# Gates of 64 more tokens through two small tables, and the gate loads issued by ScalarE

## The chip, the cores and the metric

The kernel runs on 1 core of one Trainium2 chip. The metric is the device time of one execution in microseconds (us), the median of several runs. The profile is one execution, recorded by the hardware profiler.

A core has five engines with a queue each, which run in parallel and wait for each other through semaphores: TensorE (PE in the profile; PEld are its weight loads), VectorE (DVE), ScalarE (ACT), GpSimd (POOL) and SyncE (SP), which here only issues DMAs. SyncE, ScalarE and GpSimd can issue DMAs; an issue takes its turn in the queue of its engine.

## The reference

A trunk of two layers over 256 tokens of 1024 channels, in float32. Layer 0 mixes tokens by a gated short convolution, layer 1 by windowed attention; after each mixer stands a PEER block, which is where nearly all of the time goes. A PEER block finds, for each token, 8 heads x 16 experts out of 16384, by the best sums of two sub-key scores, and computes

```python
idx = ...                                   # 128 experts per token, number i1 * 128 + i2
g = softmax(top_v, axis=-1)                 # 16 gates per head
h = einsum("cd,ced->ce", x, u_tab[idx])
a = g * gelu(h)
out = einsum("ce,ced->cd", a, v_tab[idx])
```

## The kernel before

**The PEER block is computed densely.** For all 16384 experts and all 256 tokens, `h = u x` is formed on TensorE (the tiles `ph`), GELU follows, the result is multiplied by a gate that is zero where the token did not choose the expert, and the product with `v` sums over the experts (the tiles `pv`). An expert has the number 128 i1 + i2; i1 is the partition and i2 = j the tile: tile j holds the experts of one i2 for all 256 tokens. `halves` are two buffers of 64 tiles each, `hm` for j below 64 ("half 0") and the routing scratch `sc` for j from 64 on ("half 1"), which by then is no longer needed for routing. In the profile they are called `hm` and `route`.

**Weights.** Each tile of 128 x 1024 float32 comes in through SyncE (`raw`, 4 buffers), ScalarE rounds it to `hi` (line 179, 3 buffers), VectorE forms the rest `lo` (line 180, 2 buffers). `take` and `prefetch` keep one tile ahead. Products of the parts give float32 precision: `wide_product`, `cols_product` for u, and `rows_product` for v, with 12 products of 512 columns per tile of v.

**Two ways for the gates.** For the first 128 tokens ("first tile") the gates are added into a table in device memory, `table`, 128 x 16384 with the cell (i1, i2, token): `sent` computes the places, and `scatter` (line 474) issues 16 indirect DMAs per head on GpSimd, 128 per layer, each with one cell per token. The DMAs of a head wait for those of the head before. The table is first blanked by `blank_table` (line 461), 8 transfers of 1 MB per layer on GpSimd, each waiting for the one before; in layer 0 that begins in the convolution, in layer 1 at the end of the first PEER block. The sub-keys `subk` (line 663) are loaded by GpSimd too, once the buffer `HB` is free. During the product with v, `load_gates` (line 922) loads the gates of two tiles from the table through GpSimd into one of 2 buffers, and `gated` (line 934) multiplies them in on VectorE.

For the other 128 tokens ("second tile") there is no table: `one_hots` (lines 855 to 859) forms one-hot rows of i1 and of i2 with the gate in three bfloat16 parts, for 8 tokens at a time, and `spread` multiplies them on TensorE (the tiles `pg`, 24 products for 8 tokens) and multiplies the result into `hm` on VectorE (line 871). `spread_half(0)` runs beside the u products of half 1, `spread_half(1)` beside the v products of the first 62 tiles; both calls take all 128 tokens.

**The order.** `bg` is a list of background steps with costs written by hand; `pump` issues some after each tile, so that they fill VectorE evenly, and `drain` issues the rest. In the v loop, step j copies the gated pair j + 2 to its high and low part (`split_pair`, lines 939 and 940, a ring of 4 pairs), gates pair j + 4, loads the gates of pair j + 8, and then multiplies tiles j and j + 1. `tc.issue_after(ins)` puts what is issued inside behind `ins` in the queue of `ins`'s engine; beyond that, the order inside a queue is planned by the framework from its own estimate of times, so that the queue isn't strictly in the order of the program. `keep_warm` multiplies zeros while TensorE would otherwise be idle; `blank` is both the source of the blanking and, seen as bfloat16, these zeros.

Of the kernel before, what the change touches and what calls it, by code (L numbers as in the profile page):

```python
# [17 lines left out]
P = 128  # L18
T = 256
# [10 lines left out]
LOW = -3.4e38  # L30
NEG = -1e30
FIRST, SPREAD, WARM = 20.0, 2.6, (9, 2, 2, 2, 4, 2)

# [41 lines left out]
def trunk_kernel(  # L75
# [78 lines left out]
    token = const.tile([P, 1], F32, name="token")  # L154
    G.iota(token, pattern=[[0, 1]], base=0, channel_multiplier=1, allow_small_or_imprecise_dtypes=True)

    i1T = const.tile([P, P], BF16, name="i1T")
    i2T = const.tile([P, P], BF16, name="i2T")
    gT = const.tile([P, 3, P], BF16, name="gT")
    place = const.tile([P, P], U32, name="place")  # L160
    gate = const.tile([P, P], F32, name="gate")
    stat = const.tile([P, 16], F32, name="stat")
    yb = const.tile([P, T], F32, name="yb")
    eps = const.tile([P, 1], F32, name="eps")
    V.memset(eps, EPS * D)
    blank = const.tile([P, 256], F32, name="blank")
    V.memset(blank, 0.0)
# [15 lines left out]
    def keep_warm(n):  # L183

        b = bank("u", "pwarm")
        for _ in range(n):
            matmul(b, zeros[:, :P], zeros, start=True, stop=True)

# [255 lines left out]
    table = dram.tile([P, P * P], F32, name="table")  # L444
    cells = table.rearrange("p (f o) -> (p f) o", o=1)
    ROWS = 2048
    blanked, group = [], []

# [7 lines left out]
    def blank_table(n):  # L456

        blanked[:] = [bg.behind] * n
        for i in range(P * P // ROWS):
            dst = table[:, ROWS * i : ROWS * i + ROWS].rearrange("p (a c) -> p a c", c=256)  # L460
            ins = nc.gpsimd.dma_start(dst, blank[:, None, :].to_broadcast([P, ROWS // 256, 256])).ins  # L461
            wait_for(ins, blanked[:1])
            blanked[:] = blanked[1:] + [ins]

    def scatter(h):

        earlier = blanked[:] if h == 0 else group[:]
        group.clear()
        for k in range(TOPK):
            c = slice(TOPK * h + k, TOPK * h + k + 1)  # L470

            def one():
                group.append(
                    nc.gpsimd.indirect_dma_start(  # L474
                        cells, bass.IndirectOffsetOnAxis(ap=place[:, c], axis=0), gate[:, c], None,
                        compute_op=ALU.add,
                    ).ins
                )

            if k < 2:  # L480
                one()
                wait_for(group[k], earlier)
            else:
                with tc.issue_after(group[0]):
                    one()
            for g in group[:-1]:
                tc.declare_no_dep(group[-1], g, reason="other cells")


# [169 lines left out]
    def peer(layer, last, meanwhile):  # L659
# [9 lines left out]
        scores = [sc(NSUB, P)]  # L669
        sc.at = 36 * T  # L670
        scores.append(sc(NSUB, P))
# [10 lines left out]
        sel = sc(3, P)  # L682
        small = sc(2, PH)
        turn = [0]

# [90 lines left out]
        def sent(h0, h1):  # L776
# [4 lines left out]
            for h in range(h0, h1):  # L781
                scatter(h)

# [13 lines left out]
        def routed(t, h0, h1):  # L797
# [11 lines left out]
            else:  # L809
                bg.add(1.0, turned)  # L810


# [61 lines left out]
        def spread_half(half):  # L874
            made = {}
            for t0 in range(0, P + 8, 8):
                if t0 < P:
                    bg.add(SPREAD - 0.6, one_hots, half, t0, made)
                if t0 > 0 and t0 % 16 == 0:
                    bg.add(1.2, spread, halves[half], t0 - 16, made)  # L880
# [4 lines left out]
            sc.t.rearrange("p (a t) -> p a t", a=HALF),  # L885
        ]
        for half, hm in enumerate(halves):
            if half == 1:
                spread_half(0)
                bg.plan(bg.cost(), HALF - 4)  # L890
            for j in range(0, HALF, 2):
# [15 lines left out]
                else:  # L907
                    S.activation(hm[:, j : j + 2], b.rearrange("p (a t) -> p a t", a=2), AF.Gelu)
        bg.drain()
        spread_half(1)  # L910
# [6 lines left out]

        first, gates_of, sent_last = [], {}, group[:]

        def load_gates(j):  # L920
            g = strm.tile([P, 2, P], F32, tag="gates", name="gates", bufs=2)
            load = lambda: nc.gpsimd.dma_start(g, table[:, P * j : P * j + 2 * P].rearrange("p (a t) -> p a t", a=2)).ins  # L922
            if not first:
                first.append(load())
                wait_for(first[0], sent_last)
            else:
                with tc.issue_after(first[0]):
                    first[1:] = [load()]
            gates_of[j] = g

        def gated(j, behind):
            h = halves[j // HALF][:, j % HALF : j % HALF + 2, :P]
            with tc.issue_after(behind):
                return V.tensor_tensor(h, h, gates_of.pop(j), ALU.mult).ins  # L934

        def split_pair(j):
            a = aring[:, (j // 2) % 4]
            src = halves[j // HALF][:, j % HALF : j % HALF + 2].rearrange("p a t -> p (a t)")
            S.copy(a[:, 0], src)  # L939
            return V.tensor_tensor(a[:, 1], src, a[:, 0].bitcast(F32), ALU.subtract).ins  # L940
# [10 lines left out]
        for j in range(0, P, 2):  # L951
# [9 lines left out]
            if j + 8 < P:  # L961
                load_gates(j + 8)
            a = aring[:, (j // 2) % 4]
            parts = [(a[:, 0, c], a[:, 1, c]) for c in (slice(0, T), slice(T, 2 * T))]
# [152 lines left out]
```

## Time and profile before

| | us |
|---|---|
| median of 3 runs | 1782.96 (1782.61 to 1783.4) |
| the profiled execution's own time | 1782.79 |
| its span, first to last instruction | 1780.9 |
| TensorE busy | 1766.4 |
| VectorE busy | 1367.9 |
| ScalarE busy | 930.1 |
| GpSimd busy | 575.4 |

The mean granted clock of TensorE is 0.999 of full speed. The span begins at 0 in all rows; layer 0's u products run from 160 to 531 us, its v products to 892, attention to 982, and layer 1's PEER block repeats the pattern 880 us later. "busy" counts the time in which an engine has an instruction in work; issuing a DMA is not counted. Engines overlap, so only what lies on the chain that ended last moves the end.

### The profile page before, as it was taken

The page shows a single profiled execution, that of the slowest core. Times are in us where ns is not written, and L with a number is a line of the kernel's source. Part 1 is how long each engine was busy: PE and PEld are TensorE (multiplying, and loading weights), DVE is VectorE, ACT ScalarE, POOL GpSimd, SP SyncE. Part 2 cuts the span into 40 slices and gives each one's busy share as a digit, 9 for nine tenths or more (in the row PEclk, how much of TensorE's full clock was granted, in tenths as well). Part 3 has the DMA queues.
Part 4 walks back from the last instruction along what each step waited for, and adds up shares of the span by engine and source line. Part 5 has one row for each costly group of instructions (what it writes and reads, how often), then busy time and mean ns, then how long its engine had stood idle before and what let it go on. Part 6 is the DMA issues. An engine that isn't in the chain of part 4 may idle for free.

```text
span 1780.9 us, 30030 instructions
## 1 busy us (share of the span) xinstructions
PE 1766.4 (99%) x11206; PEld 1539.0 (86%) x11209; DVE 1367.9 (77%) x2733; ACT 930.1 (52%) x1254; POOL 575.4 (32%) x421
## 2 busy tenths in 40 slices
PE   9999999999999999999999999999999999999998
PEld 7999998888898888888887999888888888888886
DVE  7877889977778787666585788898777787776665
ACT  5455555565554444444475655555555544444444
POOL 1000778777701000111010017877776000010000
PEclk9999999999999999999999999999999999999999
DMA  7965788876757666877774557887776666677774
GB/s 256 321 204 158 185 182 190 189 189 156 189 184 220 202 195 201 265 241 219 208 270 151 171 162 188 188 190 186 179 183 162 199 211 199 199 226 220 217 216 129
DMA packets 136397, 356.13 MB, mean 200 GB/s; under 512 B 49403, under 2 KB 49596, under 8 KB 135996
## 3 DMA queue, kind: packets, MB, share of 16 engines
q1 hardware_dynamic: 87120, 314.61, 58.4%
q0 software_dynamic: 48752, 39.52, 12.5%
q8 instruction: 87, 1.43, 0.4%
q14 instruction: 58, 0.48, 0.1%
q10 hardware_dynamic: 380, 0.10, 0.0%
HBM read 336.17 MB, written 17.99 MB: 199 GB/s over the span
## 4 chain that ended last, share of the span: by engine, by line
PE 98%; ACT 1%; DVE 1%; issue 0%; DVEq 0%; ACTq 0%
PE ph L110 40%; PE pv L110 39%; PE pq L110 7%; PE pg L110 3%; PE pconv L110 2%; PE psc L110 1%; PE pwo L110 1%; PE pout L110 1%; PE pgate L110 1%; PE po L110 0%; PE pk L110 0%; PE ptr L114 0%; PE pwarm L110 0%; ACT mix L592 0%; ACT xn L312 0%; PE ppt L114 0%
## 5 line engine op out<-in xcount | busy, mean ns | idle before, releaser
L180 DVE TENSOR_TENSOR lo<-raw,hi 128x1024 fp32r<-128x1024 f32 (+1 forms) x597 | 726.6, 1220 | 262.5 <-ACT hi L179 130.6
L179 ACT CAST hi<-raw 128x1024 fp32r<-128x1024 f32 (+1 forms) x597 | 625.9, 1050 | 541.6 <-PE ph L110 193.9
L474 POOL DMA_INDIRECT table<-gate,place x256 | 481.1, 1879 | 284.5 <-DVE place L780 154.5
L110 PE MATMUL ph<-xn,hi 128*128 128x512 f32 (+1 forms) x2336 | 514.5, 366 | 0.0
L110 PE MATMUL pv<-hi,xn 128*128 128x512 f32 x2048 | 508.9, 389 | 0.0
L110 PEld LDWEIGHTS pv<-hi,xn 128*128 128x128 f32 x2048 | 384.5, 188 | 80.3
L110 PEld LDWEIGHTS ph<-xn,hi 128*128 128x128 f32 x2336 | 386.9, 190 | 56.6
L110 PEld LDWEIGHTS ph<-xn,lo 128*128 128x128 f32 x2048 | 276.1, 191 | 17.2
L110 PE MATMUL ph<-xn,lo 128*128 128x256 f32 x2048 | 283.3, 282 | 0.0
L922 POOL DMA_DIRECT2D gates<-table x128 | 69.3, 541 | 662.4 <-DVE hm L934 312.7
L110 PE MATMUL pv<-lo,xn 128*128 128x512 f32 x1024 | 278.0, 391 | 0.0
L110 PEld LDWEIGHTS pv<-lo,xn 128*128 128x128 f32 x1024 | 190.9, 188 | 38.8 <-DVE lo L180 0.3
L939 ACT CAST xn<-hm 128x512 fp32r<-128x512 f32 x64 | 39.6, 622 | 89.7 <-PE pv L110 62.1
L939 ACT CAST xn<-route 128x512 fp32r<-128x512 f32 x64 | 39.9, 624 | 85.5 <-PE pv L110 83.2
L940 DVE TENSOR_TENSOR xn<-route,xn 128x512 fp32r<-128x512 f32 x64 | 44.3, 692 | 47.1 <-ACT xn L939 47.1
L859 DVE TENSOR_TENSOR oh<-oh,gT 128x512 bf16<-128x512 bf16 x192 | 69.7, 416 | 0.0
L110 PE MATMUL pq<-xr,hi 128*128 128x256 f32 x512 | 68.7, 285 | 0.3
L110 PEld LDWEIGHTS pq<-xr,hi 128*128 128x128 f32 x512 | 64.4, 192 | 2.1 <-ACT xr L312 1.7
L461 POOL DMA_DIRECT2D table<-blank x16 | 14.4, 902 | 148.7 <-DMA table<-blank 86.7
L940 DVE TENSOR_TENSOR xn<-hm,xn 128x512 fp32r<-128x512 f32 x64 | 43.9, 689 | 22.9 <-ACT xn L939 22.4
L110 PEld LDWEIGHTS <-oh 128*128 128x128 bf16 x1536 | 48.1, 97 | 4.9 <-issue 4.2
L110 PE MATMUL pg<-oh,oh 128*128 128x64 bf16 x1536 | 52.0, 193 | 0.0
(190 smaller groups left out, 1379.6 us busy)
## 6 DMA issues: line engine op xcount, KB each, us to landing
raw<-in_u SPq DMA_DIRECT2D x256, 512.0 KB, 4.0
raw<-in_v SPq DMA_DIRECT2D x256, 512.0 KB, 4.5
table<-blank POOLq DMA_DIRECT2D x16, 1024.0 KB, 7.6
raw<-in_w_q SPq DMA_DIRECT2D x32, 512.0 KB, 3.8
gates<-table POOLq DMA_DIRECT2D x128, 128.0 KB, 4.4
raw<-in_w_in SPq DMA_DIRECT2D x23, 512.0 KB, 5.1
raw<-in_w_qk SPq DMA_DIRECT2D x10, 512.0 KB, 5.8
raw<-in_w_out SPq DMA_DIRECT2D x8, 512.0 KB, 6.3
```

The lines of the kernel that those rows point to most:

```text
L110: newest[:] = [PE.matmul(*a, **k).ins]
L179: bg.rounded = S.copy(hi[:, c], raw[:, c]).ins
L180: bg.behind = V.tensor_tensor(lo[:, c], raw[:, c], hi[:, c].bitcast(F32), ALU.subtract).ins
L461: ins = nc.gpsimd.dma_start(dst, blank[:, None, :].to_broadcast([P, ROWS // 256, 256])).ins
L474: nc.gpsimd.indirect_dma_start(cells, bass.IndirectOffsetOnAxis(ap=place[:, c], axis=0), gate[:, c], None, compute_op=ALU.add,).ins
L859: V.tensor_tensor(oh2[:, 1 + j], oh2[:, 0], pairs(gT[:, j], HALF), ALU.mult)
L922: load = lambda: nc.gpsimd.dma_start(g, table[:, P * j : P * j + 2 * P].rearrange("p (a t) -> p a t", a=2)).ins
L939: S.copy(a[:, 0], src)
L940: return V.tensor_tensor(a[:, 1], src, a[:, 0].bitcast(F32), ALU.subtract).ins
```

## The change

Half 1's gates of the first 64 tokens of the second tile no longer come from one-hots but from two small tables in device memory, `far_table0` and `far_table1`, for 32 tokens ("a set") each: 128 x 4096 with the cell (i1, i2, token of the set).

- `set_apart`, after the second tile's routing, computes the places for the 64 tokens on VectorE, and eight small transfers on GpSimd lay places and gates out anew: partition = quarter of the chosen experts x token of the set, so that one indirect DMA adds 4 experts for each of 32 tokens.
- `far_additions(h, i)` issues 4 such DMAs for head h and set i, 64 per layer; each group waits for the group before of its own set. `far_pump` issues them from tile 48 of half 1 on and then in the v loop.
- `load_gates` goes to ScalarE's queue: the first behind the last rounding, the later ones behind the newest copy of `split_pair`. For tiles from 64 on, two more loads per pair, through GpSimd, bring the gates from the two tables, and `gated` multiplies them in with an operation of their own.
- `spread_half(1)` begins with token 64; `spread_half(0)` is as before.
- `blank_table` also blanks the halves of the two tables that are read, 10 transfers instead of 8; `blank` has 128 columns instead of 256, so the source of a transfer is a row of 512 bytes, repeated.
- `place` and `gate` move into the routing scratch, whose second block of scores starts 4 x 256 columns earlier. `scatter` becomes `additions`, which serves both.

```diff
 NEG = -1e30
+SET, SETS = 32, 2
 FIRST, SPREAD, WARM = 20.0, 2.6, (9, 2, 2, 2, 4, 2)
...
     G.iota(token, pattern=[[0, 1]], base=0, channel_multiplier=1, allow_small_or_imprecise_dtypes=True)
+    place_in_set = const.tile([P, 1], F32, name="place_in_set")
+    for i in range(P // SET):
+        G.iota(place_in_set[SET * i : SET * i + SET], pattern=[[0, 1]], base=0, channel_multiplier=1,
+               allow_small_or_imprecise_dtypes=True)
...
     gT = const.tile([P, 3, P], BF16, name="gT")
-    place = const.tile([P, P], U32, name="place")
-    gate = const.tile([P, P], F32, name="gate")
+    far = const.tile([P, SETS, 2 * SET], F32, name="far")
     stat = const.tile([P, 16], F32, name="stat")
...
     V.memset(eps, EPS * D)
-    blank = const.tile([P, 256], F32, name="blank")
+    blank = const.tile([P, P], F32, name="blank")
     V.memset(blank, 0.0)
...
         for _ in range(n):
-            matmul(b, zeros[:, :P], zeros, start=True, stop=True)
+            matmul(
+                b.rearrange("p (a c) -> p a c", a=2), zeros[:, :P], zeros[:, None, :].to_broadcast([P, 2, 256]),
+                start=True, stop=True,
+            )
...
     cells = table.rearrange("p (f o) -> (p f) o", o=1)
+
+    far_tables = [dram.tile([P, P * SET], F32, name=f"far_table{i}") for i in range(SETS)]
+    far_cells = [t.rearrange("p (f o) -> (p f) o", o=1) for t in far_tables]
     ROWS = 2048
-    blanked, group = [], []
+    blanked, group, far_group = [], [], [[] for _ in range(SETS)]
...
         blanked[:] = [bg.behind] * n
-        for i in range(P * P // ROWS):
-            dst = table[:, ROWS * i : ROWS * i + ROWS].rearrange("p (a c) -> p a c", c=256)
-            ins = nc.gpsimd.dma_start(dst, blank[:, None, :].to_broadcast([P, ROWS // 256, 256])).ins
+        parts = [table[:, ROWS * i : ROWS * i + ROWS] for i in range(P * P // ROWS)]
+        parts += [t[:, HALF * SET : HALF * SET + ROWS] for t in far_tables]
+        assert HALF * SET == ROWS
+        for part in parts:
+            dst = part.rearrange("p (a c) -> p a c", c=P)
+            ins = nc.gpsimd.dma_start(dst, blank[:, None, :].to_broadcast([P, ROWS // P, P])).ins
             wait_for(ins, blanked[:1])
...
-    def scatter(h):
-
-        earlier = blanked[:] if h == 0 else group[:]
+    def additions(group, columns, to, places, gates, earlier):
+
         group.clear()
-        for k in range(TOPK):
-            c = slice(TOPK * h + k, TOPK * h + k + 1)
+        for k, c in enumerate(columns):
...
                     nc.gpsimd.indirect_dma_start(
-                        cells, bass.IndirectOffsetOnAxis(ap=place[:, c], axis=0), gate[:, c], None,
+                        to, bass.IndirectOffsetOnAxis(ap=places[:, c : c + 1], axis=0), gates[:, c : c + 1], None,
                         compute_op=ALU.add,
...
                 tc.declare_no_dep(group[-1], g, reason="other cells")
+
+    def far_additions(h, i):
+
+        additions(
+            far_group[i], range(4 * h, 4 * h + 4), far_cells[i], far[:, i, :SET].bitcast(U32), far[:, i, SET:],
+            blanked[:] if h == 0 else far_group[i][:],
+        )
...
         scores = [sc(NSUB, P)]
-        sc.at = 36 * T
+        sc.at = 32 * T
         scores.append(sc(NSUB, P))
...
         small = sc(2, PH)
+
+        place, gate = sc(P, dtype=U32), sc(P)
+        apart = sc(4, 2, SET)
         turn = [0]
...
             for h in range(h0, h1):
-                scatter(h)
+                additions(
+                    group, range(TOPK * h, TOPK * h + TOPK), cells, place, gate, blanked[:] if h == 0 else group[:]
+                )
+
+        def set_apart():
+
+            n = SET * SETS
+
+            def quarters(a):
+                return a[:n].rearrange("p (h g k) -> p g h k", g=4, k=4)
+
+            def half(i):
+                return apart[:n, :, i].rearrange("p g (h k) -> p g h k", k=4)
+
+            V.scalar_tensor_tensor(linef[:n], sel[:n, 0], float(P), sel[:n, 1], op0=ALU.mult, op1=ALU.add)
+            V.tensor_scalar(
+                half(0).bitcast(U32), quarters(linef), float(SET), place_in_set[:n], op0=ALU.mult, op1=ALU.add
+            )
+            V.tensor_copy(half(1), quarters(sel[:, 2]))
+            for i in range(SETS):
+                for g in range(4):
+                    nc.gpsimd.dma_start(
+                        far[SET * g : SET * g + SET, i],
+                        apart[SET * i : SET * i + SET, g].rearrange("p a k -> p (a k)"),
+                    )
...
                 bg.add(1.0, turned)
+                bg.add(0.6, set_apart)
...
             made = {}
-            for t0 in range(0, P + 8, 8):
+            first = SET * SETS if half else 0
+            for t0 in range(first, P + 8, 8):
                 if t0 < P:
                     bg.add(SPREAD - 0.6, one_hots, half, t0, made)
-                if t0 > 0 and t0 % 16 == 0:
+                if t0 > first and t0 % 16 == 0:
                     bg.add(1.2, spread, halves[half], t0 - 16, made)
...
         ]
+        far_steps = deque((h, i) for h in range(PH) for i in range(SETS))
+
+        def far_pump():
+            if far_steps:
+                far_additions(*far_steps.popleft())
+
         for half, hm in enumerate(halves):
...
                     S.activation(hm[:, j : j + 2], b.rearrange("p (a t) -> p a t", a=2), AF.Gelu)
+                if half == 1 and j >= HALF - 16 and j % 4 == 0:
+                    far_pump()
         bg.drain()
...
-        first, gates_of, sent_last = [], {}, group[:]
+        first, gates_of, sent_last, copied = [], {}, group[:], []
...
             g = strm.tile([P, 2, P], F32, tag="gates", name="gates", bufs=2)
-            load = lambda: nc.gpsimd.dma_start(g, table[:, P * j : P * j + 2 * P].rearrange("p (a t) -> p a t", a=2)).ins
+            load = lambda: nc.scalar.dma_start(g, table[:, P * j : P * j + 2 * P].rearrange("p (a t) -> p a t", a=2)).ins
             if not first:
-                first.append(load())
+                with tc.issue_after(bg.rounded):
+                    first.append(load())
                 wait_for(first[0], sent_last)
             else:
-                with tc.issue_after(first[0]):
-                    first[1:] = [load()]
-            gates_of[j] = g
+                with tc.issue_after(copied[0] if copied else first[0]):
+                    load()
+            gates_of[j] = [(slice(0, P), g)]
+            if j >= HALF:
+                f = strm.tile([P, SETS, 2, SET], F32, tag="far_gates", name="far_gates", bufs=2)
+                for i in range(SETS):
+                    with tc.issue_after(first[0] if len(first) < 2 else first[1]):
+                        ins = nc.gpsimd.dma_start(
+                            f[:, i], far_tables[i][:, SET * j : SET * j + 2 * SET].rearrange("p (a t) -> p a t", a=2)
+                        ).ins
+                    if j == HALF:
+                        wait_for(ins, far_group[i])
+                first[1:] = [ins]
+                gates_of[j].append((slice(P, P + SETS * SET), f))
         def gated(j, behind):
-            h = halves[j // HALF][:, j % HALF : j % HALF + 2, :P]
-            with tc.issue_after(behind):
-                return V.tensor_tensor(h, h, gates_of.pop(j), ALU.mult).ins
+            for c, g in gates_of.pop(j):
+                h = halves[j // HALF][:, j % HALF : j % HALF + 2, c]
+                if c.start:
+                    h, g = h.rearrange("p a (s t) -> p a s t", s=SETS), g.rearrange("p s a t -> p a s t")
+                with tc.issue_after(behind):
+                    ins = V.tensor_tensor(h, h, g, ALU.mult).ins
+            return ins
...
             src = halves[j // HALF][:, j % HALF : j % HALF + 2].rearrange("p a t -> p (a t)")
-            S.copy(a[:, 0], src)
+            copied[:] = [S.copy(a[:, 0], src).ins]
             return V.tensor_tensor(a[:, 1], src, a[:, 0].bitcast(F32), ALU.subtract).ins
...
                 load_gates(j + 8)
+            far_pump()
             a = aring[:, (j // 2) % 4]
```

## Rows read from the trace of the kernel before

**Rows 1.** The page's part 1: busy us, share of the span, instructions.
```profile
PE 1766.4 (99%) x11206; PEld 1539.0 (86%) x11209; DVE 1367.9 (77%) x2733; ACT 930.1 (52%) x1254; POOL 575.4 (32%) x421
```

**Rows 2.** The chain that ended last: start us, us, what.
```profile
118.00 1.60 PE psc L110 x12
...
531.39 24.51 PE pv L110 x108
555.90 1.47 PE pg L110 x48
557.37 21.89 PE pv L110 x96
...
705.77 1.47 PE pg L110 x48
707.24 182.82 PE pv L110 x806
```

**Rows 3.** Groups by line: busy us, mean ns | idle before, releasers.
```profile
L180 DVE TENSOR_TENSOR lo<-raw,hi 128x1024 fp32r<-128x1024 f32 (+1 forms) x597 | 726.6, 1220 | 262.5 <-ACT hi L179 130.6 <-PE ph L110 83.3 <-issue 25.5
...
L859 DVE TENSOR_TENSOR oh<-oh,gT 128x512 bf16<-128x512 bf16 x192 | 69.7, 416 | 0.0
```

**Rows 4.** Lines 934 (ns min/median/max, first, last start) and 922 (landing us).
```profile
L934 DVE TENSOR_TENSOR route<-route,gates x64: 407/419/420, 700.5 to 1746.4; 128x256 f32<-128x256 f32 x64
...
DMA to landing us min/median/max: 2.3/4.4/5.6
```

**Rows 5.** Line 474: ns min/median/max, first and last start, landing.
```profile
L474 POOL DMA_INDIRECT table<-gate,place x256: 1532/1648/2613, 181.9 to 1365.2; - x128
...
DMA to landing us min/median/max: 2.9/4.7/8.2
```

**Rows 6.** Timeline of GpSimd, layer 0: start us, us, what [idle before].
```profile
484.94 2.43 POOL L474 DMA_INDIRECT table<-gate,place  x1 [0.31 <-issue]
491.03 1.20 POOL L922 DMA_DIRECT2D gates<-table  x2 [3.65 <-DMA table<-gate,place]
```

**Rows 7.** Timeline of 505 to 560 us, around the start of pv.
```profile
518.59 0.58 ACT L234 COPY route<-ph 128x512 f32<-128x512 f32 x1
...
524.76 1.05 ACT L179 CAST hi<-raw 128x1024 fp32r<-128x1024 f32 x1 [1.75 <-PE ph L110]
...
528.60 0.75 DVE L934 TENSOR_TENSOR hm<-hm,gates 128x256 f32<-128x256 f32 x2
...
529.75 1.14 ACT L939 CAST xn<-hm 128x512 fp32r<-128x512 f32 x2
```

**Rows 8.** Timeline of GpSimd, 0 to 345 us: blanking and subk.
```profile
34.08 0.94 POOL L461 DMA_DIRECT2D table<-blank  x1 [2.22 <-DMA table<-blank]
...
84.42 0.89 POOL L461 DMA_DIRECT2D table<-blank  x1 [7.21 <-DMA table<-blank]
103.74 0.57 POOL L663 DMA_DIRECT2D route<-in_subk  x1 [18.44 <-PE pout L110]
```

**Rows 9.** DMA queues, 25 to 103 us (8 blanks), then 107 to 108.
```profile
q0 software_dynamic: 2208, 8.42, 30.9%
...
DMA packets 50, 0.41 MB, mean 410 GB/s; under 512 B 0, under 2 KB 0, under 8 KB 0
```

**Rows 10.** Timeline of ScalarE, first 40 us: a DMA issue in its queue.
```profile
0.73 0.41 ACTq L145 DMA_DIRECT2D gain<-in_gains  x1
```

**Rows 11.** Timeline of 740 to 757 us, pv without one-hots.
```profile
739.82 0.62 ACT L939 CAST xn<-route 128x512 fp32r<-128x512 f32 x1 [1.44 <-PE pv L110]
...
741.08 0.42 DVE L934 TENSOR_TENSOR route<-route,gates 128x256 f32<-128x256 f32 x1
```

**Rows 12.** DMA issues of the whole span: KB each, us to landing.
```profile
gain<-in_gains ACTq DMA_DIRECT2D x1, 16.0 KB, 3.3
```

**Rows 13.** Timeline of 560 to 574 us, pv behind a spread.
```profile
560.02 0.62 ACT L939 CAST xn<-hm 128x512 fp32r<-128x512 f32 x1 [3.03 <-PE pv L110]
...
565.77 0.42 DVE L934 TENSOR_TENSOR hm<-hm,gates 128x256 f32<-128x256 f32 x1
```

## The prediction, made before the change was run

> **What bounds the kernel now.** I read the page's busy shares first, then the chain that ended last, then the lines and stretches that the diff touches. TensorE is busy for 99% of the span, VectorE for 77%, ScalarE for half, GpSimd for a third [rows 1]. The chain runs through TensorE without a break in the stages that count: in the second product of a PEER layer ("pv", activations times `v`) pieces of pv and of pg, the one-hot products of `spread`, follow each other back to back [rows 2]. So a product taken from TensorE there is time taken away, as long as nothing else becomes late. The argument is the 12 us that leave, and then five covers that have to hold.
>
> **What the change removes.** `spread_half(1)` starts at token 64 of the second tile instead of 0. A piece of pg is one pair of `spread` calls (16 tokens, 48 products) and takes 1.47 us [rows 2]; a layer has 8 pieces in half 1 and keeps 4, so 8 go in two layers: 8 x 1.47 = 11.76 us. A piece has a small echo: eight tiles of pv behind one take 21.89 us, 2.736 a tile, while the stretch without pg takes 182.82 us for 806 products, 2.722 per 12 [rows 2]. That is 0.11 us for each of the 8 pieces, 0.9 us. Gross gain: 12.6 us.
>
> VectorE loses, per layer, 8 calls of `one_hots` (three of the five operations of a call take 3 x 0.42 us [rows 3], so over 10 us) and 8 evictions. It gains 32 multiplications in the second half of pv, half the size of the present ones at 0.42 us [rows 4], so at most 13 us, where no one-hots run; the three operations of `set_apart` go among the u products. None of it lies on the chain, so the relief counts nothing; if VectorE's slack were gone, the new work would cost what is left of those 13 us.
>
> **GpSimd's additions.** 64 per layer, behind the 128 that are there. Those began at 181.9, the last at 484.9, and the gates were loaded at 491.0, once it had landed [rows 5, 6]: 2.38 us each, waits included. Eight `set_apart` transfers (each at most the 0.6 us of a gates load [rows 6]: 5 us) and 64 x 2.38 = 152 us end at about 648 us. Pair 64 was first gated at 700.5 [rows 4], now some 6 us earlier, 694. At the longest addition seen, 2.61 us, plus 0.31 to the next [rows 5, 6], and no group waits, it is 491 + 5 + 64 x 2.92 = 683. A group of four waits for the last group of its own set, with a group of the other set between (4 x 2.4 = 9.5 us), and the slowest landing was 8.2 us [rows 5]; so I price these waits at nothing, and rival three at what they cost uncovered. The DMA time of the additions now falls beside the v loads; beside the u loads the chain shows no wait for weights, so nothing for that.
>
> The Trainium skill's "SBUF — State Buffer", section "Who interferes with whom", says that a VectorE instruction with two SBUF inputs contends with a GpSimd instruction that reads SBUF, and that the later one is blocked until the first is through. Additions of 1.53 to 2.61 us for the same work [rows 5] agree with it; by that rule the far additions go to the long end, beside the one-hots of pv, and the time is still the one below.
>
> `place` and `gate` move to columns 59.7 to 60.7 (in units of 256) of the routing scratch, where half 1 writes pairs 58 and 60 of `hm`. Pair 58 was written at 518.6 [rows 7]; the additions that read the tables had landed by 491 [rows 6], and `set_apart`'s transfers would by about 501. Covered by 17 us: nothing.
>
> **Blanking.** Ten 1 MB transfers per layer instead of eight, read from a row of 512 bytes where it was 1 KB. Each waits for the one before: the second at 34.08 us, the eighth at 84.42, 8.39 apart [rows 8]. Behind them in GpSimd's queue the `subk` load went out at 103.74 [rows 8]; at 107 to 108 it was moving 410 GB/s alone, which puts its 1 MB at some 5 us, 108.5 [rows 9]. TensorE's psc, which reads it, has its first long piece at 118.0 [rows 2]. At the old pace the tenth blank starts at 34.08 + 8 x 8.39 = 101.2 and nothing moves. No row shows transfers with 512-byte rows, so bounds: the same pace, or twice the engine time. Eight blanks took 30.9% of 78 us, 24.1 us for 8.42 MB: 3.0 us per MB, 349 GB/s of their own time against the 410 of `subk`, whose rows are 8 KB [rows 9]. If the pieces make that difference, halving them adds some 17%, 0.5 us. I take a pace of 8.9, nearest to that: tenth at 105.3, `subk` landed near 114. Nothing lost, with 3 to 4 us of cover left. In layer 1 `subk` waits for its buffer until long after the blanks.
>
> **Loads on ScalarE.** One issue is 0.41 us in the queue [rows 10], 64 per layer are 26 us, on an engine that is idle half the time. What counts is the wait inside: a load waits for the gating that frees its buffer, two pairs ahead of it, and roundings may stand behind it. In the plain stretch a pair's copy ends at 740.44 and that gating at 741.50 [rows 11], so a rounding comes up to 1.5 us late. A rounding starts when TensorE frees its buffer; its tile is two tiles or 5.4 us off, of which rounding and difference take 1.05 [rows 7] and 1.22 [rows 3]. Room of 3.1 us covers 1.5.
>
> The thin place is the start of pv. Before, gates had been in since 496, gating ran at 528.60, the copies to 530.89, and pv began at 531.39 [rows 2, 6, 7]. Now the first load stands behind the last rounding, which ends at 525.8 [rows 7]. The old loads landed after 2.3 to 5.6 us [rows 4], a ScalarE load after 3.3 [rows 12]: gates are in from 528.1 to 531.4, and gating, perhaps one more issue, and one copy take 1.4 us. So pv starts between on time and 1.5 us late; I take 0.4 us, near the ScalarE landing, 0.8 in two layers.
>
> **Sum.** 1780.9 - 12.6 + 0.8 = 1769.1 us of span; the profiled execution's own time has 1.9 us around the span and lies 0.2 under the median of 1782.96. So 1771.2 us; a start of pv 0 to 1.5 us late gives 1770.4 to 1773.4.
>
> **Rivals.** One, slower: blanking from short rows costs twice the engine time, 3 us more. The pace is 11.4, the tenth starts at 125, `subk` lands near 134, psc waits 16 us: 1787 us. It begins to cost at a pace of 9.4, and outweighs the gain from 10.8. For it: blanks already fill a third of DMA beside the weights [rows 9]. Against it: 349 against 410 GB/s leaves little that can be due to pieces. A rule bears on it. The Trainium skill's "DMA: Bandwidth & Descriptors", section "Why small descriptors are slow (HBM only)", adds about 3 cycles to one cycle per 32 bytes: an estimate of 38 for 35 when a piece is halved, 9%; by it the pace is 8.7 and the rival is out. No run here shows such rows yet.
>
> Two: ScalarE's wait makes weights late where VectorE is held up by one-hots. At a spread the gating ended 5.6 us after the copy (560.64 to 566.19 [rows 13]), 2.5 past the room: 8 spreads x 2.5 = 20 us, 1791 us. Against it: VectorE rounded off two tiles between these two, and that needs ScalarE's roundings, so no load can stand ahead of them; what is left is some 0.5 us each, 1775 us.
>
> Three: the far additions wait group by group for landings, 3.7 us as the last did [rows 6], 16 times: 59 us more, 707, gates landed near 711, VectorE stuck at pair 64 from 694; less the room and what lies ahead, about 10 us a layer, 1791 us. The alternating sets speak against it.
>
> Four: the removed pieces limited nothing: 1783 us. The unbroken chain speaks against it.
>
> **How the numbers follow.** Less than 0.2% (3.6 us) can hardly be told from no change here. Likeliest, all covers hold: 0.71, 1770 to 1774. Part of a cover fails (rival one at a pace of 9.4 to 10.8, rival two in its small form, more at the start of pv): 0.12, from 1774 to 1782, two thirds of it under 1779.4. Rival one in full 0.05, two in full 0.03, three 0.06, all slower; four 0.03. Faster 0.71 + 0.08 = 0.79; same 0.04 + 0.03 = 0.07; slower 0.14. A range of 1769.6 to 1780.5 holds the first case and most of the second.
>
> **What would show it.** Right: 24 pieces of pg on the chain instead of 32; pv still 2.72 to 2.74 us a tile; at most 1 us of ScalarE or VectorE on the chain where pv begins; the additions over by 650 us; `subk` out by 107 us. Wrong: psc behind a wait for `subk` near 118 us; roundings behind gates' loads in ScalarE's queue, with gaps of TensorE in pv; VectorE idle ahead of the gating of pair 64.

## The result, and the profile after

| | before | after |
|---|---|---|
| median, us | 1782.9 (6 runs, 1782.5 to 1783.4) | 1770.86 (6 runs, 1769.5 to 1772.9) |
| ratio to before | | 0.9932 [0.9922, 0.9942] |
| profiled execution, us | 1782.8 | 1770.06 |
| its span, us | 1780.9 | 1768.3 |

The kernel became 0.7% faster; the profiled span is 12.6 us shorter. The forecast was 1771.2 us, and 1769.1 us for the span. The sum held; its step on blanking did not, as the runs below show.

Busy times of the changed kernel, the line that answers [rows 1]:

```profile
PE 1753.7 (99%) x10825; PEld 1527.9 (86%) x10825; DVE 1343.2 (76%) x2707; ACT 929.7 (53%) x1254; POOL 855.6 (48%) x573
```

TensorE lost 12.7 us of work and is still busy for 99% of the span, so nothing has taken its place as the bound. GpSimd gained 280 us, and the chain has none of them.

The chain of the changed kernel in pv of layer 0 (start us, us, what), against [rows 2]:

```profile
531.46 51.74 PE pv L111 x228
583.19 1.47 PE pg L111 x48
...
672.17 24.61 PE pv L111 x108
696.77 1.47 PE pg L111 x48
698.24 185.54 PE pv L111 x818
...
889.20 5.96 PE pk L111 x44
...
1405.33 51.74 PE pv L111 x228
...
1572.11 183.03 PE pv L111 x806
```

and the ends of pv in the chain of the kernel before, which [rows 2] leave out:

```profile
895.48 5.96 PE pk L110 x44
...
1411.60 24.51 PE pv L110 x108
...
1587.45 180.30 PE pv L110 x794
```

Four pieces of pg are left in pv (583.19, 625.59, 670.70, 696.77), 24 in the whole chain where there were 32. From the first product of pv to the first of the next stage, `pk`, layer 0 took 531.39 to 895.48 before, 364.09 us, and takes 531.46 to 889.20 now, 357.74: 6.35 us less. Layer 1, from its first pv to the end of pv, took 1587.45 + 180.30 - 1411.60 = 356.15 before and takes 1572.11 + 183.03 - 1405.33 = 349.81 now: 6.34 less. Together 12.69, and between them nothing else moved: pv starts at 531.46 where it started at 531.39.

Where pv begins, by the timeline (start us, us, engine line, what):

```profile
524.82 1.05 ACT L183 CAST hi<-raw 128x1024 fp32r<-128x1024 f32 x1 [1.75 <-PE ph L111]
525.13 0.35 ACTq L977 DMA_DIRECT2D gates<-table  x1
...
528.66 0.42 DVE L1004 TENSOR_TENSOR hm<-hm,gates 128x256 f32<-128x256 f32 x1
...
529.75 0.43 DVE L1004 TENSOR_TENSOR hm<-hm,gates 128x256 f32<-128x256 f32 x1 [0.67 <-DMA gates<-table]
529.81 0.62 ACT L1010 CAST xn<-hm 128x512 fp32r<-128x512 f32 x1
```

The first load leaves behind the last rounding, and gating runs at 528.66, as it did before (528.60 in [rows 7]). Only the second gating waits for its gates, 0.67 us, and the copy is still in time for pv.

GpSimd's timeline, first the blanking, then the additions of layer 0:

```profile
35.26 1.19 POOL L474 DMA_DIRECT2D table<-blank  x1 [3.73 <-DMA table<-blank]
...
105.30 1.15 POOL L474 DMA_DIRECT2D far_table<-blank  x1 [8.59 <-DVE xr L327]
106.44 0.56 POOL L681 DMA_DIRECT2D route<-in_subk  x1
...
505.21 1.64 POOL L485 DMA_INDIRECT far_table<-far  x1 [2.44 <-DMA far<-route]
...
640.94 1.54 POOL L485 DMA_INDIRECT far_table<-far  x1 [0.30 <-issue]
...
646.34 1.65 POOL L990 DMA_DIRECT2D far_gates<-far_table  x3 [3.22 <-DMA far_table<-far]
```

The second to the tenth blank is 8 steps: (105.30 - 35.26) / 8 = 8.76 us a blank, against 8.39 in [rows 8]. (The row of the tenth names VectorE as what ended its wait; by the DMA queues the ninth's last packets moved until after 104 us, and by the program it waits for the ninth. The pace differs from profile to profile: 8.03 in run one with rows of 1 KB, 8.27 to 9.01 in runs two and seven to eleven with 512 bytes.) The 64 far additions run from 505.21 to 642.48, 2.145 us each. The line that gates pair 64 (ns min/median/max, first and last start us) shows what is left of the cover:

```profile
L1004 DVE TENSOR_TENSOR route<-route,far_gates x64: 281/284/286, 690.0 to 1734.1; 128x128 f32<-128x128 f32 x64
```

The far gates of pair 64 are asked for at 642 and 646, a load from each table, and multiplied in at 690.

One place lost a little, the start of the routing scores. The chain there:

```profile
107.59 1.24 DVE lo L184
108.85 7.52 DMA raw<-in_w_q
...
116.47 1.05 ACT hi L183
117.52 0.49 ACT route L867
...
118.05 1.60 PE psc L111 x12
```

Before, TensorE ran through this place without a wait. Now psc stands behind ScalarE's copy of the queries that it multiplies (from `pq`), that behind a rounding, and that behind a weight of `w_q` that took 7.5 us to land. Run seven below follows it up.

### The profile page after: what moved, and what is told of

Same layout as the page of the kernel before. It is cut to its first block, busy times and chain, and to the rows that moved or that the text cites. A ratio compares the mean times of both kernels' runs of the same rounds, so it can differ in the third digit from the quotient of the medians.

```text
span 1768.3 us, 29799 instructions
## 1 busy us (share of the span) xinstructions
PE 1753.7 (99%) x10825; PEld 1527.9 (86%) x10825; DVE 1343.2 (76%) x2707; ACT 929.7 (53%) x1254; POOL 855.6 (48%) x573
## 4 chain that ended last, share of the span: by engine, by line
PE 97%; ACT 1%; DVE 1%; DMA 0%; issue 0%; ACTq 0%; DVEq 0%
PE ph L111 41%; PE pv L111 39%; PE pq L111 6%; PE pconv L111 2%; PE pg L111 2%; PE psc L111 1%; PE pwo L111 1%; PE pout L111 1%; PE pgate L111 1%; PE po L111 0%; DMA raw<-in_w_q 0%; PE pk L111 0%; PE ptr L115 0%; PE pwarm L111 0%; ACT hi L183 0%; ACT mix L610 0%
## 5 line engine op out<-in xcount | busy, mean ns | idle before, releaser
L485 POOL DMA_INDIRECT table<-route x256 | 501.5, 1959 | 276.2 <-DVE route L801 152.5
L485 POOL DMA_INDIRECT far_table<-far x128 | 242.6, 1895 | 43.4 <-issue 35.3
L990 POOL DMA_DIRECT2D far_gates<-far_table x128 | 70.1, 552 | 342.6 <-DVE route L1004 329.0
L474 POOL DMA_DIRECT2D table<-blank x16 | 18.7, 1170 | 146.1 <-DMA table<-blank 63.4
L905 DVE TENSOR_TENSOR oh<-oh,gT 128x512 bf16<-128x512 bf16 x144 | 52.4, 421 | 0.1
L959 ACT ACTIVATE route<-route 128x512 f32<-128x512 f32 x62 | 39.0, 629 | 17.7 <-DVE route L242 8.5
```

The lines of the kernel that those rows point to most:

```text
L485: nc.gpsimd.indirect_dma_start(to, bass.IndirectOffsetOnAxis(ap=places[:, c : c + 1], axis=0), gates[:, c : c + 1], None, compute_op=ALU.a ...
L905: V.tensor_tensor(oh2[:, 1 + j], oh2[:, 0], pairs(gT[:, j], HALF), ALU.mult)
L959: S.activation(hm[:, j : j + 2], hm[:, j : j + 2], AF.Gelu)
L990: ins = nc.gpsimd.dma_start(f[:, i], far_tables[i][:, SET * j : SET * j + 2 * SET].rearrange("p (a t) -> p a t", a=2)).ins
```

## The experiments

**One: the loads alone.** The kernel before, with its gates' loads issued by ScalarE as in the changed kernel, and all 16 calls of `one_hots` still beside pv.

```
-   load = lambda: nc.gpsimd.dma_start(g, ...)
+   load = lambda: nc.scalar.dma_start(g, ...)
-       first.append(load())
+       with tc.issue_after(bg.rounded):
+           first.append(load())
...
-       with tc.issue_after(first[0]):
+       with tc.issue_after(copied[0] if copied else first[0]):
```

> The kernel before with one part of the change: gates' loads in ScalarE's queue, the first behind the last rounding. No small tables; all 8 pieces of pg of half 1 stay. If the gain is the pg pieces that leave and nothing else: no change, 1783 us within 0.1% (up to 0.8 us slower if the gates come late at the start of pv). If moving the loads off GpSimd brought part of the gain: 2 us or more faster, 1781 or less. If ScalarE's wait made weights late behind the one-hots (rival two, now with 16 spreads): 1787 or more, with gaps of TensorE in pv.

1784.91 us (10 runs), ratio 1.0010 [1.0001, 1.0020]; the span is 2.0 us longer than before. Timeline of TensorE, in pv:

```profile
542.69 1.20 PE L110 MATMUL pv<-lo,xn 128*128 128x512 f32 x4 [0.46 <-DVE lo L180]
```

and of VectorE at the same time:

```profile
540.40 1.10 DVE L859 TENSOR_TENSOR oh<-oh,gT 128x512 bf16<-128x512 bf16 x3
541.41 1.23 DVE L180 TENSOR_TENSOR lo<-raw,hi 128x1024 fp32r<-128x1024 f32 x1
```

TensorE waits for a difference that stands behind one-hots on VectorE. Up to the first piece of pg, layer 0 lost 0.82 us by this and layer 1 0.88. Another 0.46 us near 720 belongs to this version alone: there a step of the attention's preparation loses its hold behind GpSimd's loads, and the gating of one pair comes late. So the loads by ScalarE gain nothing themselves, and with the old load on VectorE they cost 0.85 us a layer.

**Two: half the dose.** One table of 32 tokens instead of two.

```
-SET, SETS = 32, 2
+SET, SETS = 32, 1
```

> The changed kernel with SETS = 1: half the dose, 32 tokens through one small table, spread_half(1) from token 32. If the time goes with pg pieces at 1.58 us each: 2 pieces a layer leave instead of 4, so half the gain, 6.3 us: 1776.6 us, between 1775.5 and 1778. If the gain came from the other edits (loads moved, VectorE lighter): nearly the whole gain stays, 1772 or less. Blanking is 9 transfers, so subk starts near 104 us and no late weight of w_q.

1777.12 us (6 runs), ratio 0.9966 [0.9953, 0.9978]: 28 pieces of pg, half the dose and about half the gain.

**Three: the gates' loads back on GpSimd**, with the rest of the change kept.

```
-   load = lambda: nc.scalar.dma_start(g, ...)
+   load = lambda: nc.gpsimd.dma_start(g, ...)
-       with tc.issue_after(bg.rounded):
-           first.append(load())
+       first.append(load())
...
-       with tc.issue_after(copied[0] if copied else first[0]):
+       with tc.issue_after(first[0]):
```

> The changed kernel with gates' loads back in GpSimd's queue. In the order planned for that queue the first two loads stand ahead of the 64 far additions and the third load behind them. If the move to ScalarE is what keeps the additions out of the way: pair 4 waits for the end of the additions, from about 542 to between 630 and 655 us, so 88 to 113 us lost in each layer: 1947 to 1997 us, with TensorE idle in pv. If the move does not matter: 1771 us.

1984.5 us (one run). Its waits of TensorE (us in total, times, longest):

```profile
PE pv L111 <- DVE lo L184: 208.7, 2, 104.5
```

The loads that pv needs stand behind the far additions in GpSimd's queue, and pv stands still for 104 us a layer. Moving the loads to another queue is what the far tables need in order to cost nothing, not a gain of its own.

**Four: the first load not held behind the last rounding.**

```
-       with tc.issue_after(bg.rounded):
-           first.append(load())
+       first.append(load())
```

> The changed kernel, but the first gates' load of a layer is not held behind the last rounding; the plan then puts it behind the 106th rounding, at about 312 us by the trace, while the last addition to the table lands near 503. If ScalarE's queue really stands still for a load that waits: TensorE runs out of weights from about 320 us until the additions end, which is sooner than 503 because VectorE is idle then (470 to 500): 150 to 190 us a layer, 2070 to 2150 us in all. If a waiting load lets later roundings pass: 1771 us.

2052.9 us (one run), with this wait in each layer:

```profile
PE ph L111 <- DVE hm L242: 276.7, 2, 138.9
```

The load goes into ScalarE's queue early, waits there for GpSimd's additions, and all of ScalarE's work waits behind it, 139 us a layer. Less than expected (150 to 190 us); the mechanism is that of rival two, at the price it has where nothing hides it.

**Five: shorter rows.** The blanks read rows of 256 bytes where the changed kernel reads 512.

```
-   dst = part.rearrange("p (a c) -> p a c", c=P)
-   ins = nc.gpsimd.dma_start(dst, blank[:, None, :].to_broadcast([P, ROWS // P, P])).ins
+   dst = part.rearrange("p (a c) -> p a c", c=64)
+   ins = nc.gpsimd.dma_start(dst, blank[:, None, :64].to_broadcast([P, ROWS // 64, 64])).ins
```

> The changed kernel with blanking read from rows of 256 bytes instead of 512 (same bytes, same ten transfers). Rows of 1 KB went at a pace of 8.39 us, rows of 512 bytes at 8.76. If a fixed time per piece sets this (0.37 us for 8192 more pieces a transfer's worth of halving): the next halving adds about twice that, pace 9.5, tenth blank at 111.3 us, subk landing near 121, and psc, due at 118, waits 3 to 4 us: 1774 to 1775 us, layer 1 unchanged. If rows cost nothing and 8.76 was contention: pace 8.8 and 1771. If rival one's price (time in proportion to pieces) held: pace over 12, psc 20 us late, 1790 or more.

1790.9 us (4 runs), ratio 1.0045 [1.0030, 1.0061]: the end that rival one named, one halving later. GpSimd's timeline:

```profile
38.49 1.73 POOL L474 DMA_DIRECT2D table<-blank  x1 [6.41 <-DMA table<-blank]
...
123.23 1.69 POOL L474 DMA_DIRECT2D far_table<-blank  x1 [9.22 <-DMA far_table<-blank]
124.90 0.57 POOL L681 DMA_DIRECT2D route<-in_subk  x1
```

and TensorE's wait:

```profile
PE psc L111 <- DMA route<-in_subk: 17.6, 1, 17.6
```

The pace is (123.23 - 38.49) / 8 = 10.59 us, between two of the expected values, and `subk` lands 10.3 us after its issue. Psc is done 19.3 us later than without a wait, and that is the loss. Of it 17.6 us are the wait; behind it the granted clock is 0.5 (the lower level, 1.2 GHz) up to 138.7 us, TensorE having stood idle since 118, and the 16 products of psc take 3.65 us where the chain before has 0.45 and 1.60.

**Six: far additions as one chain.** Each group of four waits for the group right before it, whichever its set.

```
-    blanked, group, far_group = [], [], [[] for _ in range(SETS)]
+    blanked, group, far_group, far_newest = [], [], [[] for _ in range(SETS)], []
...
-            blanked[:] if h == 0 else far_group[i][:],
+            blanked[:] if h == 0 and i == 0 else far_newest[:],
...
+        far_newest[:] = far_group[i]
```

> The changed kernel, but each group of four far additions waits for the group right before it, whichever set, instead of the last group of its own set. If the landing between groups is what the alternation hides (rival three): about 4 us of idle GpSimd at each of 16 groups, additions over at 700 instead of 642 us, the gating of pair 64 at about 708 instead of 690, and TensorE waits 8 to 14 us in each layer: 1787 to 1799 us. If the waits are short or VectorE has more room there: 1771 to 1775 us.

1804.05 us (one run). GpSimd's timeline where the additions end:

```profile
703.80 1.54 POOL L485 DMA_INDIRECT far_table<-far  x1 [0.30 <-issue]
```

VectorE and TensorE behind them:

```profile
709.83 0.29 DVE L1005 TENSOR_TENSOR route<-route,far_gates 128x128 f32<-128x128 f32 x1 [18.99 <-DMA far_gates<-far_table]
...
711.32 2.08 PE L111 MATMUL pv<-lo,xn 128*128 128x512 f32 x4 [16.53 <-DVE lo L184]
```

The additions end at 705, where rival three had put them (707), and GpSimd's waits for landings are 115 us in 29 places of the two layers, 4.0 each. VectorE stands for 19 us at pair 64 with the differences of weights behind it, and TensorE loses 16.5 us here and 12.9 in the other layer. The prediction had allowed 10: the room ahead of the gating is less than it took.

**Seven: the far blanks behind `subk`.** The two far tables are blanked after `subk` has been issued instead of ahead of it.

```
-        parts += [t[:, HALF * SET : HALF * SET + ROWS] for t in far_tables]
...
-        nc.gpsimd.dma_start(sk, subk[layer])
+        with tc.issue_after(nc.gpsimd.dma_start(sk, subk[layer]).ins):
+            blank_parts([t[:, HALF * SET : HALF * SET + ROWS] for t in far_tables])
```

> The changed kernel with the two blanks of the small tables issued behind the subk load instead of ahead of it. In the changed kernel the tenth blank and subk together kept a w_q weight waiting 7.5 us for its landing and cost TensorE 0.3 to 0.4 us at 118 us in the profiled execution. If that collision is all that is lost and what scatters the times: subk out at 104 us, no wait before psc, 0.4 us of span back and a smaller spread: 1770.0 to 1770.6 us. If the two blanks only collide with the next weights instead: same time within 1 us.

1770.6 us (5 runs, 1770.05 to 1770.96), ratio 0.9929 [0.9915, 0.9942]. The chain:

```profile
80.75 19.52 PE pout L111 x86
...
118.08 1.60 PE psc L111 x12
```

No weight and no copy stands on it: from pout to the first long piece of psc 118.08 - 80.75 = 37.33 us, as before (118.00 - 80.67 = 37.33). The changed kernel takes 118.05 - 80.34 = 37.71.

The burst in GpSimd's queue is not gone: a blank still leaves right behind `subk`, at 104.42, and by the DMA queues GpSimd's has the engines alone from 105 to 111 us. But the weights' packets resume between 111 and 112, and in the changed kernel only between 113 and 114. So it seems to count when the burst ends; that was not tried by itself.

**Eight: one-hots that nobody reads.** VectorE makes the one-hots of the dropped calls as well; no product uses them.

```
-            for t0 in range(first, P + 8, 8):
+            for t0 in range(0, P + 8, 8):
```

> VectorE also makes the one-hots of the eight calls per layer that the change dropped; nothing reads them and no product of pg comes back, so only VectorE's relief is undone. If that relief counts nothing: 1770.9 us, within 1 us. If it is the relief that lets pv begin without a loss (the loads alone on ScalarE lost 0.85 us per layer there, with TensorE waiting for a difference at 542.7): some 1.7 us more, 1772.6, and TensorE waits for `lo` between 538 and 546 us in layer 0.

1771.33 us (5 runs, 1770.2 to 1772.2), ratio 0.9932 [0.9919, 0.9946]. By times of runs this can't be told from the changed kernel (1770.54 beside it). The chain is finer:

```profile
532.08 13.72 PE pv L111 x60
545.83 87.33 PE pv L111 x384
...
634.63 24.61 PE pv L111 x108
...
890.21 5.95 PE pk L111 x44
```

Pv of layer 0 takes 358.13 us instead of 357.74, with a break at 545.8 where TensorE waits for VectorE; layer 1 takes 350.09 instead of 349.81, with a break at 1419.9. Together 0.67 us: between the two values expected, nothing and 1.7. In both places the difference that TensorE waits for stands behind one-hots on VectorE. But a break of this size is no proof of one-hots: in run ten's profile the changed kernel, without them, loses 0.33 us at 542.2 in layer 0 (pv takes 358.07), behind gates that landed late.

**Nine: the products alone come back.** Each kept piece makes its 48 products twice.

```
-            for t in range(8):
+            for t in [t for t in range(8) for _ in range(1 + (hm is halves[1]))]:
```

> Each of the four pieces of pg that half 1 keeps per layer makes its 48 products twice (the second writing over the first), with no more one-hots and no more evictions. If what the change gained is TensorE's time alone: 8 x 1.47 = 11.8 us come back, 1782.6. If part of the 12.6 us belongs to VectorE's relief, or to the echo behind each piece (0.11 us x 8), that part stays gained: 1781.7 or less.

1782.89 us (11 runs), ratio 0.9998 [0.9989, 1.0007]. The chain:

```profile
533.50 51.84 PE pv L111 x228
585.34 2.92 PE pg L111 x96
...
678.68 24.61 PE pv L111 x108
...
897.17 5.94 PE pk L111 x44
```

Pv of layer 0 takes 363.67 us, 5.93 more than in the changed kernel, and of layer 1 355.60, 5.79 more: 11.72, the 8 x 1.47 of the removed pieces and nothing beside them. Pv stays 0.97 us shorter than in the kernel before; the medians, 1782.89 and 1783.38 for the kernel before beside it, are too coarse to show that. (In this profile pv also starts 2 us later, 533.50 against 531.46: pout began 1.1 us later, and the wait that the next run shows took the rest.)

**Ten and eleven: the changed kernel and run seven's version once more, side by side.**

> The changed kernel beside the next, for one comparison on one chip: 1770.9 us. If the queue's burst of the tenth blank and `subk` at 108 to 112 us costs what it seemed to (0.35 to 0.4 us), it is that much behind the version with the far blanks behind `subk`; if not, level with it.

> The version with the far blanks behind `subk`, once more: 1770.5 us if the burst costs 0.4 us in the changed kernel, 1770.9 if it does not.

1770.54 us (5 runs, 1770.2 to 1772.9) and 1770.41 us (5 runs, 1769.4 to 1772.8). By time they are level. The chain of the changed kernel's profile in this run:

```profile
81.19 19.52 PE pout L111 x86
...
109.67 9.24 DMA raw<-in_w_q
...
119.01 1.04 ACT hi L183
120.06 0.49 ACT route L867
...
120.59 1.61 PE psc L111 x12
```

This time a weight took 9.2 us and psc starts 120.59 - 81.19 = 39.40 us behind pout, 2.07 more than without a wait. This profile is of the slowest of the five executions, and that of the other version, with no wait here, of the fastest; of the 3.4 us between their spans 2.1 are this wait, 1.1 the start of pout and 0.3 the break at the start of pv. Nine profiles side by side:

| version | tenth blank (or last ahead of `subk`) starts, us | pout to psc, above 37.33 us |
|---|---|---|
| before (8 blanks ahead) | 84.4 | 0 |
| far blanks behind `subk`, two profiles | 89.8, 89.0 | 0, 0 |
| one table (9 blanks ahead) | 98.9 | 0 |
| one-hots kept | 102.3 | 0 |
| changed | 105.3 | 0.38 |
| products doubled | 107.7 | 1.37 |
| changed, again | 108.0 | 2.07 |
| rows of 256 bytes | 123.2 | 19.3 (to the end of psc) |

The loss begins when the last blank ahead of `subk` starts after 102 to 105 us and grows from there.

## Why the prediction was right, and where not

**The gain.** Predicted 12.6 us gross, measured 12.69 in pv. The 11.76 of it for eight pieces is settled by run nine, which brings back 11.72 with products alone. The other 0.9 us the prediction read as a small echo behind each piece, and that holds. Nine tiles with no piece ahead of them take 24.51 us (from 531.39 in [rows 2]); nine tiles behind a piece take 24.61, in the changed kernel, in run eight and in run nine alike, whether VectorE makes half of the one-hots or all of them, and whether the piece has 48 products or 96. By the timelines it lies in the first four products behind a piece, which take 1.17 us where four such products take 1.07 elsewhere; why is not shown. Eight echoes of 0.10 to 0.11 us left with eight pieces; run nine adds no piece, so they do not come back there.

VectorE's relief was to count nothing, and in the gain it does not: the kernel before has all the one-hots and no break at the start of pv. Run eight shows it as a cost avoided: with the loads on ScalarE and all the one-hots, up to 0.67 us in two layers, in one break near the start of each pv.

**The start of pv.** Predicted 0.4 us late a layer, measured 0 in the profile after and 0.33 in layer 0 of run ten's. Gates were in hand about when the prediction had them at the earliest. The thin place is some 10 us later, and it is VectorE's: run one loses 0.85 us a layer there with all the one-hots. By run eight the one-hots explain 0.3 to 0.4 us of a layer's loss; the rest of run one's loss, the pieces' own evictions or the gates' timing, stays open.

**The far additions.** Predicted over at 648, measured 642.5, by two errors of which one hid the other. They began at 505.2 and not 496, because the additions to `table` ended 11 us later than before (498.7 against 487.4; why was not tried). And they went at 2.145 us each, against 2.38; the groups of their own set made GpSimd wait for only 3.0 us in the two layers, 10 times. Nor did they go to the long end of the durations, as the prediction had expected beside the one-hots: one takes 1.90 us in the mean, one to `table` 1.96. Gating of pair 64 came at 690, predicted 694. Runs three and six show both ways in which this cover fails, at 104 and at 13 to 17 us a layer. Rival three's mechanism and its end of the additions were right, its price too low by a third.

**Loads on ScalarE.** No wait of TensorE in pv is left in the profile after, so the room covered the loads' waits. Run four shows what rival two's mechanism costs uncovered.

**Blanking: the step that failed.** The pace was near (8.9 predicted, 8.76 measured), and `subk` went out at 106.4 (by 107 predicted). That the tenth blank started at 105.3, as predicted, is in part luck: the second came 1.2 us later than in the kernel before, and the pace made up for it. `subk` itself was in time; by the DMA queues nearly all of it had moved by 114. But "nothing lost, with 3 to 4 us of cover left" was wrong: 0.4 to 2.1 us were lost in the three profiles with rows of 512 bytes whose tenth blank started at 105 us or later (in the medians of runs ten and eleven it does not show). The prediction followed only `subk` to its reader. It did not ask what else a blank and `subk` back to back keep from the DMA engines: a weight in SP's queue, with ScalarE's rounding behind it, and behind that the copy that psc reads.

The threshold of rival one was too kind as well. It was to cost from a pace of 9.4, 8 us for each us of pace, so 9.5 us at run five's 10.59; the run lost 19.3. Most of the difference lies in three places: the second blank began at 38.49 and not at 34.08, since the first was slower too (4.4 us); `subk` landed 12.0 us after the start of the tenth blank, where the rival had 9 (3.0 us); and psc's products ran at a granted clock of 0.5 behind the wait (1.6 us).

**The sum.** Predicted span 1769.1; in its place 1780.9 - 12.69 + 0 at the starts of pv + 0.38 ahead of psc - 0.33 since pout started that much earlier (80.34 against 80.67) = 1768.3, the measured one. The start of pout lies between 80.1 and 81.4 in these profiles, whichever version, so this last term is scatter.

## What to carry to other kernels

When a product can be replaced by data that another engine prepares, the gain is the product's own time on the bound, and everything else is a question of covers: check each by what it costs when it fails. Follow a longer burst in one DMA queue not only to its own reader but to every transfer of the other queues that is issued while it lasts. And two effects of nearly the same size, here 0.9 us behind pieces and 0.67 us behind one-hots, are told apart by the place in the chain where they stand, not by comparing totals.

## What the runs showed of the hardware

Row size. Blanks of 1 MB from rows of 1 KB, 512 and 256 bytes keep a pace of 8.39, 8.76 and 10.59 us each beside the same weights. Their own DMA time, the queue's share of the engines by the bytes it moved, is 30.9% x 78 / 8.42 = 2.86 us per MB in [rows 9], and by these lines (queue, packets, MB, share, over 35 to 105 us) 38.3% x 70 / 8.41 = 3.19 for the changed kernel

```profile
q0 software_dynamic: 2192, 8.41, 38.3%
```

and 39.7% x 70 / 6.46 = 4.30 for run five:

```profile
q0 software_dynamic: 1714, 6.46, 39.7%
```

In these profiles the first halving adds 12%, the second 35%. But the same reckoning gives 2.92 for run one, with 1 KB, and 2.82 to 3.42 for runs two and seven to eleven, with 512 bytes, so the first halving is lost in the scatter; only run five's 4.30 lies clear of it. The Trainium skill's "DMA: Bandwidth & Descriptors", section "Why small descriptors are slow (HBM only)", gives by estimate 9% for the first, from its 3 cycles a packet, and 44 for 38, 16%, for the second: the first lies within the scatter, and the trace shows more than the second.

For some us one queue has all the engines. In the changed kernel a weight was asked for at 108.85 in SP's queue. The DMA queues from 108 to 112 us have one line:

```profile
q0 software_dynamic: 243, 1.07, 102.2%
```

GpSimd's queue, with a blank and `subk` in it, had all engines, and the weights' queue (q1) not a packet. The Trainium skill's "DMA: Bandwidth & Descriptors", section "Queues, rings and completion order", has each engine take turns between the queues it has work for, packet by packet; these 4 us don't show such turns. Whether the weight's descriptors had reached the engines by then no view tells.

A load that waits in ScalarE's queue stops the engine behind it: 139 us a layer in run four.

Additions go faster where the other engines stand still. In run three, from 555 to 630 us, VectorE, ScalarE and TensorE do nothing, and a far addition takes 1.54 or 1.55 us, 1.85 us after the one before; in the changed kernel they take 1.55 to 4.14 us and come 2.145 us apart. Whether VectorE or the weights' transfers make the difference was not tried.
